# A chunk-wise LRU head with its adaLN sums beside the first blocks, and a Hyena convolution with packed outer stages and rows asked for ahead

## The chip, the cores and the metric

The kernel runs on one core of one Trainium2 chip. The metric is device time in microseconds, the median of three runs. In the rows, PE is TensorE's matrix work, PEld its weight loads, DVE VectorE, ACT ScalarE, POOL GpSimd and SP SyncE; SPq and ACTq are DMA queues by the engine that issues them.

## The reference, cut to what matters

```python
for i in range(DEPTH):                      # DEPTH 2: layer 0 RG-LRU, layer 1 Hyena
    sh1, sc1, g1, sh2, sc2, g2 = split(silu(c) @ ada_w[i] + ada_b[i], 6)   # context: silu(c_ctx)
    u = rms_norm(x, norm_g[i, 0]) * (1 + sc1) + sh1
    ...
    x = x + g1 * y                          # y from the mixer
    x = x + g2 * (relu(modulate(x, ..., sh2, sc2) @ w1) ** 2 @ w2)
# RG-LRU: z = u @ w_in + b_in; gate = gelu(z[:W]); xl = conv4(z[W:]) by rows of 64
# r, i = sigmoid(xl @ w_a), sigmoid(xl @ w_i) by heads, two directions; scans; (hf + hb) * gate @ w_out
# Hyena: z = conv3(u @ w_in + b_in); v, x1, x2 = split(z, 3)
v = x1 * long_conv(v, k_f[:, 0], skip[0])   # long_conv: irfft(rfft(v, 2L) * k_f)[:L] + v * skip
v = x2 * long_conv(v, k_f[:, 1], skip[1])
return v @ w_out + b_out
```

D is 1024, there are 1024 latent tokens (two chunks of 512, c = 0 and 1) and 256 context tokens (chunk c = 2).

## The kernel before, in words

**Products.** A float32 product of the GEMMs is made of three passes on rounded operands: `mm3` (L135 to L137) multiplies whi by uh, whi by ul and wlo by uh. `load` brings a weight block of 512 KB into one of two `raw` buffers (L113), ScalarE rounds it to `whi` (L115), VectorE makes the rest `wlo` (L117). `gemm2` (L154) does two chunks side by side. The Hyena convolution multiplies in full float32: such a matmul of 512 columns is two instructions in the trace.

**Head.** `filter_pos` computes the features of the Hyena filter. `ada_first` (L160 to L185) makes the shift and scale sums of both conditionings (M=2, one PSUM tile for each half, L174) for j = 0 and 1, eight weight tiles each, and transposes the two rows of the result (L181). `norm_apply` modulates the three chunks: a multiply on VectorE (L288), the modulation on ScalarE (L290), the rounding on ScalarE (L291), the rest ul on VectorE or GpSimd (L292). Then the list `TOKENS` (L472) gives the order of the LRU's work: Xhm is an input block (all three chunks with one weight, then a convolution along the tokens on VectorE, L527, and its rounding), Zhm a gate block, Uhm the recurrent gates, Ejx the gate sum j of adaLN: eight 512 KB tiles weighted and added on VectorE (L659, L661), then reduced over partitions by matmuls (L664).

**Hyena long convolution.** Four units u (order o, chunk c) of 16 row blocks. `s1` (L864) turns V into the first transform stage, one 128x128 float32 matmul for each half m of block g; ScalarE copies it to `e` (L866) and a DMA puts it into eight rows of `BIG[u]`, rows `prow(2g+m)` and every fourth behind it. A loop over 64 steps does `fstep` (the filter's spectrum ft by L974, the signal's by L979, four VectorE products L983 to L986, one GpSimd sum L993) and, LAG = 3 steps later, `bstep` (L998, ScalarE copy L999 back to BIG). `s2p` fetches the rows of BIG by DMA (tile e2, L957) and multiplies them by `md` (L958). Inside unit u, the list `side` holds s2p of unit u-1 (8 calls) and s1 of unit u+1 (8 calls), spread over the steps; unit 3 has `back` (transposes L1015 and products L1016) in place of s1. s1 of unit 0 sits in the in-projection before the loop, s2p of unit 3 and half of `back` in the out-projection behind it.

## Time and profile before

| | |
|---|---|
| median of 3 runs | 2819.17 us (2819.03 to 2819.62) |
| profiled execution | 2820.53 us |
| its span | 2818.8 us |
| PE busy | 2664.5 us, 95% |
| DVE / ACT / POOL busy | 1519.5 / 1045.7 / 256.6 us |

The span is the time between the first and the last recorded instruction; 1.73 us of the profiled execution lie around it. Where PE is busy the whole time, only less work on PE can shorten a stretch; where it stands, the row of the next matmul names what it waited for.

### The profile page before, as it was taken

The page shows a single profiled execution, that of the slowest core. Times are in us where ns is not written, and L with a number is a line of the kernel's source. Part 1 is how long each engine was busy: PE and PEld are TensorE (multiplying, and loading weights), DVE is VectorE, ACT ScalarE, POOL GpSimd, SP SyncE. Part 2 cuts the span into 40 slices and gives each one's busy share as a digit, 9 for nine tenths or more (in the row PEclk, how much of TensorE's full clock was granted, in tenths as well). Part 3 has the DMA queues.
Part 4 walks back from the last instruction along what each step waited for, and adds up shares of the span by engine and source line. Part 5 has one row for each costly group of instructions (what it writes and reads, how often), then busy time and mean ns, then how long its engine had stood idle before and what let it go on. Part 6 is the DMA issues. An engine that isn't in the chain of part 4 may idle for free. (4 is left out here: it accounts for less than half of the span.)

```text
span 2818.8 us, 30100 instructions
## 1 busy us (share of the span) xinstructions
PE 2664.5 (95%) x11578; PEld 2027.9 (72%) x11578; DVE 1519.5 (54%) x2077; ACT 1045.7 (37%) x1566; POOL 256.6 (9%) x162
## 2 busy tenths in 40 slices
PE   6689898999999999999999998889799999999998
PEld 1577777878777777778787763333588888888887
DVE  7665665874554554554843447547485333333336
ACT  5557577552333333322622233323353221112213
POOL 0223333010000000000100013212000000000000
PEclk8789999999999999999999999999999999999999
DMA  8331122342443443431313235555421111111112
GB/s 302 124 123 40 50 75 100 117 129 75 135 134 114 142 133 110 135 114 57 120 56 111 83 123 150 139 162 160 134 83 48 51 47 51 45 53 45 53 45 97
DMA packets 120272, 286.28 MB, mean 102 GB/s; under 512 B 11898, under 2 KB 27900, under 8 KB 120002
## 3 DMA queue, kind: packets, MB, share of 16 engines
q1 hardware_dynamic: 109618, 261.30, 29.5%
q10 hardware_dynamic: 8256, 14.68, 1.8%
q0 software_dynamic: 2256, 8.39, 0.9%
q8 instruction: 91, 1.49, 0.2%
q14 instruction: 51, 0.42, 0.0%
HBM read 212.76 MB, written 37.75 MB: 89 GB/s over the span
## 5 line engine op out<-in xcount | busy, mean ns | idle before, releaser
L154 PE MATMUL ps<-u,whi 128*128 128x512 f32 x2696 | 733.5, 392 | 0.0
L115 ACT CAST whi<-raw 128x1024 fp32r<-128x1024 f32 x206 | 216.7, 1052 | 1130.8 <-PE ps L154 1033.5
L154 PEld LDWEIGHTS ps<-u,whi 128*128 128x128 f32 x2696 | 504.1, 188 | 114.6 <-DVE x L789 4.2
L117 DVE TENSOR_TENSOR wlo<-raw,whi 128x1024 fp32r<-128x1024 f32 x206 | 262.1, 1272 | 468.7 <-ACT whi L115 467.9
L154 PE MATMUL ps<-u,wlo 128*128 128x512 f32 x1348 | 421.3, 389 | 0.1
L154 PEld LDWEIGHTS ps<-u,wlo 128*128 128x128 f32 x1348 | 252.9, 188 | 53.7 <-DVE wlo L117 0.8
L154 PE MATMUL ps<-hh,whi 128*128 128x512 f32 x896 | 290.6, 393 | 0.0
L154 PE MATMUL ps<-hh,wlo 128*128 128x512 f32 x896 | 288.4, 389 | 0.0
L154 PE MATMUL ps<-hl,whi 128*128 128x512 f32 x896 | 287.7, 390 | 0.0
L154 PEld LDWEIGHTS ps<-hh,whi 128*128 128x128 f32 x896 | 168.2, 188 | 51.4 <-DVE x L789 11.1
L136 PE MATMUL ps<-u,whi 128*128 128x512 f32 (+1 forms) x508 | 195.4, 386 | 3.7 <-POOL u L292 3.1
L135 PE MATMUL ps<-u,whi 128*128 128x512 f32 (+1 forms) x508 | 187.3, 385 | 11.5 <-ACT u L291 11.5
L137 PE MATMUL ps<-u,wlo 128*128 128x512 f32 (+1 forms) x508 | 193.1, 382 | 1.8 <-DVE wlo L117 1.8
L154 PEld LDWEIGHTS ps<-hh,wlo 128*128 128x128 f32 x896 | 168.1, 188 | 35.2
L154 PEld LDWEIGHTS ps<-hl,whi 128*128 128x128 f32 x896 | 167.9, 188 | 33.8
L789 DVE SCALAR_TENSOR_TENSOR big<-ps,mod,big 128x512 f32<-128x512 f32 (+1 forms) x132 | 91.7, 731 | 185.2 <-PE ps L154 177.7
L789 DVE SCALAR_TENSOR_TENSOR x<-ps,mod,x 128x512 f32<-128x512 f32 x128 | 91.4, 747 | 132.8 <-PE ps L154 124.9
L415 DVE TENSOR_TENSOR ht<-ps,ht 128x512 f32<-128x512 f32 x64 | 44.0, 687 | 162.9 <-PE ps L137 162.9
L292 POOL TENSOR_TENSOR u<-nu,u 128x512 fp32r<-128x512 f32 x24 | 33.9, 1412 | 990.6 <-ACT u L291 981.4
L135 PEld LDWEIGHTS ps<-u,whi 128*128 128x128 f32 x508 | 98.0, 194 | 30.1 <-ACT u L291 12.3
L136 PEld LDWEIGHTS ps<-u,whi 128*128 128x128 f32 x508 | 98.2, 193 | 25.6 <-POOL u L292 6.4
L137 PEld LDWEIGHTS ps<-u,wlo 128*128 128x128 f32 x508 | 97.7, 192 | 20.3 <-DVE wlo L117 3.0
(228 smaller groups left out, 3798.2 us busy)
## 6 DMA issues: line engine op xcount, KB each, us to landing
raw<-in_mlp_w_dram SPq DMA_DIRECT2D x136, 512.0 KB
adaw<-in_ada_w_dram SPq DMA_DIRECT2D x112, 256.0 KB
fd<-fe SPq DMA_DIRECT2D x64, 256.0 KB
ft<-fd SPq DMA_DIRECT2D x64, 256.0 KB
e<-big SPq DMA_DIRECT2D x64, 256.0 KB
eraw<-in_ada_w_dram SPq DMA_DIRECT2D x24, 512.0 KB
raw<-in_hy_w_in_dram SPq DMA_DIRECT2D x24, 512.0 KB
big<-e ACTq DMA_DIRECT2D x48, 256.0 KB
```

What stands on the lines that cost most here:

```text
L115: lsplit[0] = nc.scalar.copy(hi, raw)
L117: lsplit[1] = nc.vector.tensor_tensor(lo, raw, hi.bitcast(F32), op=ALU.subtract)
L135: first = pin(nc.tensor.matmul(ps, wh, rh, start=start, stop=False))
L136: pin(nc.tensor.matmul(ps, wh, rl, start=False, stop=False))
L137: pin(nc.tensor.matmul(ps, wl, rh, start=False, stop=stop))
L154: nc.tensor.matmul(pp[c], x, y[c][k], start=first, stop=last)
L292: applied[k % 2] = (nc.vector if k % 2 else nc.gpsimd).tensor_tensor(ul[k], u, uh[k].bitcast(F32), op=ALU.subtract)
L415: nc.vector.tensor_tensor(ht, ps, ht, op=ALU.mult)
L789: last[0] = nc.vector.scalar_tensor_tensor(xs[m][:, cs], ps[:, :n], g2[:, m:m + 1], xs[m][:, cs], op0=ALU.mult, op1=ALU.add)
```

## The change

It has two halves.

**LRU head.** `ada_first` puts four M=2 matmuls of a pair of weight tiles at four places in one PSUM tile (rows 0, 32, 64, 96), and `finish` adds the halves. Loads come in the order x chunk 0, adaLN tiles and the other chunks; three weight blocks are split at once, and the token B00 takes the place of X00, X01 and Z00: chunk by chunk, for each k three blocks. Half of the tiles of chunk 0 (a quarter of the others) are modulated on VectorE. The filter's matrix `hp` is built later, in `filter_mat`; the fourth filter weight is no longer split ahead and kept in DRAM, but at each use. The sum j = 3 (F, G) lies inside B, j = 4 behind U00, and j = 2 (E00 to E30, in halves of 512) at the end of the LRU.

**Hyena.** `s1` and `s2p` take a pair of blocks gp at a time, as eight matmuls of 32 rows by 64 columns and of 64 rows by 32 columns of the array. The matrix of `back` becomes a permutation (a float32 matmul instead of a transpose), `prow` and the layouts of V and of the convolution change to fit, with more and shorter VectorE and ScalarE operations in `use`. `s2load` asks for the rows of two pairs ahead at step LAG, with 12 buffers (4 in the out-projection, asked for at the use); ft is asked for 3 steps ahead with 4 buffers (8 before); the DMAs into BIG all go to SP's queue (before: ACT's in the loop).

```diff
 def prow(g):
-    return 32 * (g >> 2) + (g & 3)
+    return 64 * (g & 1) + 32 * (g >> 3) + (g >> 1 & 3)
...
+            for i in (0, 1):
+                for h in range(2):
+                    r = 64 * i + 32 * h
+                    nc.tensor.matmul(pp[j][r:r + 2, :], cond[:, :, k - 1 + i], ws[k - 1 + i][:, h * 512:(h + 1) * 512], start=(k == 1), stop=(k == NT - 1))
...
+                if inplace and (k % 2 == 0 if even else k % 4 == 1):
+                    nc.vector.tensor_scalar(u, t, scale[:, k:k + 1], shift[:, k:k + 1], op0=ALU.mult, op1=ALU.add)
+                else:
+                    nc.scalar.activation(u, t, AF.Identity, scale=scale[:, k:k + 1], bias=shift[:, k:k + 1])
...
-    TOKENS = ("X00 X01 E20 Z00 E30 U00 E40 A00 X10 S00 Z01 U01 A01 X11 S01 "
+    TOKENS = ("B00 U00 F40 G40 A00 X10 S00 Z01 U01 A01 X11 S01 "
...
-              "Z30 U30 A30 Z31 U31 " + " ".join(f"Y{k}{c}" for k in range(6) for c in range(2)) + " S30 A31 S31")
+              "E00 Z30 E10 U30 A30 Z31 E20 U31 E30 " + " ".join(f"Y{k}{c}" for k in range(6) for c in range(2)) + " S30 A31 S31")
...
+            def B(h, m):
...
+                for c in range(3):
+                    n = 3 if c < 2 else 2
...
+                    for k in range(NT):
+                        for i in range(n):
+                            mm[0] = gemm(pp[i], w0[i], 0, uh[c], ul[c], [k], NT)
...
+                F(3, 0)
+                for i in range(2):
+                    mix(0, i, zz[i])
+                G(3, 0)
...
-            def s2p(u, g):
+            rows_ = {}
+
+            def s2load(u, gp, pool=cA, bufs=12):
+
+                ee = rows_[u, gp] = []
+                for n in range(2):
+                    for m in range(2):
+                        e = pool.tile([P, 512], F32, tag="e2", name=nm("e2"), bufs=bufs)
+                        b = prow(4 * gp + 2 * n + m)
+                        nc.sync.dma_start(e, BIG[u][b:b + 29:4])
+                        ee.append(e)
+
+            def s2p(u, gp):
...
+                for r in range(2):
+                    rows = slice(64 * r, 64 * r + 64)
+                    for n in range(2):
+                        for m in range(2):
+                            k = 2 * m + r
+                            k = 3 - k if n else k
+                            pin(nc.tensor.matmul(po[n][32 * k:32 * k + 32], md[rows], ee[2 * n + m][rows], start=True, stop=True))
...
-                        pin(nc.tensor.transpose(pt[:, gg * P:(gg + 1) * P], V[c][:, 4 * g4 + gg, j * P:(j + 1) * P], ident))
+                        pin(nc.tensor.matmul(pt[:, gg * P:(gg + 1) * P], V[c][:, 4 * g4 + gg, j * P:(j + 1) * P], pm[:, gg % 2], start=True, stop=True))
...
+                            def both(u, g):
+                                if g == 0:
+                                    s2load(u, 2)
+                                elif g == 1:
+                                    s2load(u, 3)
+                                s2p(u, g)
+                            side += [lambda g=g, u=u: both(u - 1, g) for g in range(4)]
...
+                    if f == LAG and u:
+                        s2load(u - 1, 0)
+                        s2load(u - 1, 1)
...
+                    s2load(3, m, cp[0], 4)
+                    s2p(3, m)
```

The next two pieces are TensorE's order in the head. In the kernel before, each row is an instruction (with the tile that it writes, the tile that it streams or holds, and the output's size): the end of X01, the j = 2 sum's matmuls into pst, the start and end of Z00, the j = 3 sum, the start and end of U00, and the j = 4 sum ahead of X10's context chunk.

```order
L137 MATMUL ps_177_843<-u_143_504,wlo_173_788 128x256
L664 MATMUL pst_190_907<-ones_77,eacc_181_882 128x1 x8
L135 MATMUL ps_195_924<-u_104_465,whi_192_919 128x512
L136 MATMUL ps_195_924<-u_112_473,whi_192_919 128x512
...
L137 MATMUL ps_196_950<-u_127_488,wlo_193_921 128x512
L664 MATMUL pst_206_1001<-ones_77,eacc_197_976 128x1 x8
L135 MATMUL ps_211_1018<-xh_169_780,whi_208_1013 128x512
L136 MATMUL ps_211_1018<-xl_170_782,whi_208_1013 128x512
...
L137 MATMUL ps_220_1083<-xh_179_878,wlo_209_1015 128x256
L664 MATMUL pst_233_1140<-ones_77,eacc_224_1115 128x1 x8
L135 MATMUL ps_240_1172<-u_136_497,whi_237_1167 128x256
```

In the changed kernel, B's first rows, its last, the j = 3 sum ahead of U00 and the j = 4 sum ahead of X10:

```order
L135 MATMUL ps_165_699<-u_2_116,whi_101_338 128x512
L135 MATMUL ps_166_700<-u_2_116,whi_104_344 128x512
L135 MATMUL ps_167_701<-u_2_116,whi_107_350 128x512
L136 MATMUL ps_165_699<-u_10_124,whi_101_338 128x512
L137 MATMUL ps_165_699<-u_2_116,wlo_102_340 128x512
L136 MATMUL ps_166_700<-u_10_124,whi_104_344 128x512
...
L137 MATMUL ps_172_856<-u_41_155,wlo_105_346 128x256
L762 MATMUL pst_188_958<-ones_77,eacc_173_907 128x1 x8
L135 MATMUL ps_193_975<-xh_183_941,whi_190_970 128x512
...
L137 MATMUL ps_202_1040<-xh_186_954,wlo_191_972 128x256
L762 MATMUL pst_215_1097<-ones_77,eacc_206_1072 128x1 x8
L135 MATMUL ps_222_1129<-u_34_148,whi_219_1124 128x256
```

Three weight blocks (whi_101, whi_104, whi_107) now share each u, and two sums instead of three stand between the first GEMM and X10.

In the loop, the rows of TensorE around the first s2p of a middle unit stand in this order before (y is a step's product, mi its inverse matrix, m21 a forward one):

```order
L974 MATMUL ps_2383_12660<-ft_2382_12658,m21_12183 128x512
L979 MATMUL ps_2385_12664<-big_2188_12181,m21_12183 128x512
L958 MATMUL ps_2389_12674<-e2_2390_12675,md_12194 128x512
L958 MATMUL ps_2389_12674<-e2_2391_12678,md_12194 128x512
L958 MATMUL ps_2393_12683<-e2_2394_12684,md_12194 128x512
L958 MATMUL ps_2393_12683<-e2_2395_12687,md_12194 128x512
L998 MATMUL ps_2396_12691<-y_2364_12615,mi0_12186 128x512
L974 MATMUL ps_2398_12696<-ft_2397_12694,m21_12183 128x512
```

And in the changed kernel, with L1122 for the filter's spectrum, L1133 for the signal's, L1152 for the inverse and L1101 for s2p (the four rows shown are the first of eight):

```order
L1122 MATMUL ps_2396_12931<-ft_2371_12875,m21_12421 128x512
L1152 MATMUL ps_2398_12935<-y_2362_12854,mi0_12424 128x512
L1133 MATMUL ps_2399_12938<-big_2192_12419,m21_12421 128x512
L1122 MATMUL ps_2404_12950<-ft_2379_12894,m21_12421 128x512
L1101 MATMUL pst_2410_12962<-e2_2383_12903,md_12432 32x512
L1101 MATMUL pst_2410_12962<-e2_2384_12905,md_12432 32x512
L1101 MATMUL prb_2411_12963<-e2_2385_12907,md_12432 32x512
L1101 MATMUL prb_2411_12963<-e2_2386_12909,md_12432 32x512
L1152 MATMUL ps_2413_12975<-y_2370_12873,mi0_12424 128x512
L1133 MATMUL ps_2414_12978<-big_2192_12419,m21_12421 128x512
L1122 MATMUL ps_2419_12990<-ft_2395_12929,m21_12421 128x512
```

Four full matmuls for two blocks have become eight small ones, in the two PSUM tiles that pst and prb use; the filter's spectrum stands one step ahead of the signal's.

SP's queue at the same place, before, with L970 for the filter's rows and L957 for those of BIG:

```order
L970 DMA ft_2452_12832<-fd_81 128x512
L970 DMA ft_2468_12871<-fd_81 128x512
L957 DMA e2_2390_12675<-big_2041_11178 128x1x512
L957 DMA e2_2391_12678<-big_2041_11178 128x1x512
L957 DMA e2_2394_12684<-big_2041_11178 128x1x512
L957 DMA e2_2395_12687<-big_2041_11178 128x1x512
L957 DMA e2_2405_12711<-big_2041_11178 128x1x512
L957 DMA e2_2406_12714<-big_2041_11178 128x1x512
L970 DMA ft_2484_12910<-fd_81 128x512
L970 DMA ft_2500_12949<-fd_81 128x512
L957 DMA e2_2408_12719<-big_2041_11178 128x1x512
L957 DMA e2_2409_12722<-big_2041_11178 128x1x512
```

And in the changed kernel (L1116 and L1087):

```order
L1116 DMA ft_2395_12929<-fd_80 128x512
L1116 DMA ft_2403_12948<-fd_80 128x512
L1087 DMA e2_2383_12903<-big_2053_11372 128x1x512
L1087 DMA e2_2384_12905<-big_2053_11372 128x1x512
L1087 DMA e2_2385_12907<-big_2053_11372 128x1x512
...
L1087 DMA e2_2409_12960<-big_2053_11372 128x1x512
L1116 DMA ft_2418_12988<-fd_80 128x512
L1087 DMA e2_2421_12994<-big_2053_11372 128x1x512
```

The rows of BIG came in sixes and fours between filter rows; now twelve stand in one piece, and the next filter row waits behind them.

## Rows read from the trace of the kernel before

**Rows 1.** The page, part 1: busy time, share of the span, instructions.

```profile
PE 2664.5 (95%) x11578; PEld 2027.9 (72%) x11578; DVE 1519.5 (54%) x2077; ACT 1045.7 (37%) x1566; POOL 256.6 (9%) x162
```

**Rows 2.** Windows: PE, PEld, DVE, ACT, POOL busy; granted clock, DMA share, GB/s.

```profile
0.00:80.00 80.00, 45.56 (x113) 13.26 (x114) 53.36 (x140) 50.80 (x88) 3.34 (x8) 0.80 0.78 272
80.00:171.00 91.00, 72.00 (x313) 60.08 (x312) 61.19 (x56) 37.64 (x62) 19.96 (x14) 0.78 0.48 150
171.00:480.00 309.00, 279.10 (x1302) 232.81 (x1303) 195.12 (x130) 210.74 (x249) 105.12 (x35) 0.94 0.19 60
...
1664.00:1983.40 319.40, 275.53 (x608) 113.02 (x606) 202.28 (x295) 106.99 (x187) 82.82 (x67) 0.95 0.55 159
```

**Rows 3.** The same view, two short windows.

```profile
6.50:42.00 35.50, 25.15 (x63) 7.63 (x64) 24.75 (x71) 19.43 (x35) 0.00 (x0) 0.84 1.03 383
2012.00:2016.00 4.00, 4.00 (x19) 3.12 (x18) 1.23 (x1) 1.40 (x3) 0.00 (x0) 1.00 0.70 225
```

**Rows 4.** Timeline of PE in the head: start, duration, group [idle before <- releaser].

```profile
79.60 1.22 PE L135 MATMUL ps<-u,whi 128*128 128x512 f32 x2 [11.54 <-ACT u L291]
...
144.90 0.77 PE L135 MATMUL ps<-xh,whi 128*128 128x512 f32 x1
...
159.93 0.39 PE L136 MATMUL ps<-xl,whi 128*128 128x512 f32 x1
160.15 0.39 PE L137 MATMUL ps<-xh,wlo 128*128 128x512 f32 x1
...
167.56 3.54 PE L664 MATMUL pst<-ones,eacc 128*128 128x1 f32 x16 [6.31 <-DVE eacc L661]
170.97 0.56 PE L135 MATMUL ps<-u,whi 128*128 128x256 f32 x1
```

**Rows 5.** Timeline of ACT before the first GEMM.

```profile
66.86 10.68 ACT L290 ACTIVATE xl<-xl,mod,scl 128x512 f32<-128x512 f32 x15 [0.67 <-DVE scl L303]
```

**Rows 6.** Lines of DVE, 0 to 300 us: count | busy, mean ns | idle <- releasers.

```profile
L527 DVE SCALAR_TENSOR_TENSOR xc<-z,vec,xc 128x1008 f32<-128x1008 f32 (+3 forms) x30 | 34.3, 1154 | 0.2
L661 DVE SCALAR_TENSOR_TENSOR eacc<-eraw,cond,eacc 128x1024 f32<-128x1024 f32 x21 | 28.9, 1376 | 21.8 <-DMA eraw<-in_ada_w_dram 21.5 <-DVE xc L527 0.2
```

**Rows 7.** Timeline of PE at the filter's packed stage.

```profile
702.83 1.09 PE L432 MATMUL ps<-ht,mf 32*32 32x512 f32 x16
703.85 0.50 PE L154 MATMUL ps<-hh,whi 128*128 128x512 f32 x1
```

**Rows 8.** Timeline of PE in the convolution loop.

```profile
1664.49 1.02 PE L979 MATMUL ps<-big,m 128*128 128x512 f32 x2
1665.35 1.88 PE L864 MATMUL ps<-v,m 128*128 128x512 f32 x4
...
1722.72 1.02 PE L979 MATMUL ps<-big,m 128*128 128x512 f32 x2
...
1725.29 1.02 PE L979 MATMUL ps<-big,m 128*128 128x512 f32 x2
...
1733.02 1.02 PE L979 MATMUL ps<-big,m 128*128 128x512 f32 x2
...
1771.56 1.02 PE L979 MATMUL ps<-big,m 128*128 128x512 f32 x2
...
1812.65 1.02 PE L979 MATMUL ps<-big,m 128*128 128x512 f32 x2
...
1906.07 1.02 PE L979 MATMUL ps<-big,m 128*128 128x512 f32 x2
```

**Rows 9.** Waits of PE, 0 to 300 and 1664 to 1983: total, times, longest.

```profile
PE pst L664 <- DVE eacc L661: 17.1, 3, 6.3
...
PE ps L958 <- DMA e<-big: 24.9, 23, 5.0
```

**Rows 10.** Timeline of PE in the out-projection.

```profile
2035.54 1.03 PE L1015 MATMUL ps<-ident,v 128*128 128x128 f32 x8
2036.33 0.71 PE L154 MATMUL ps<-yh,whi 128*128 128x512 f32 x2
```

More of the change, by code (lines that the diff above doesn't have):

```diff
@@ L96, in tile_block @@
     hpd = dram.tile([16, P, 2, P], F32, name="hpd")
-    w4d = dram.tile([4, P, 2, 512], F32, name="w4d")
     fd = dram.tile([4, 16, P, 512], F32, name="fd")
@@ L187, in ada_half @@
+        return [lambda j=j, k=k: step(j, k) for j in range(2) for k in range(NT)], finish
     def ada_half(pool, l, j, h):
@@ L387, in fetch @@
             w = fp.tile([P, 2, 512], F32R, tag="w4", name=nm("w4"), bufs=2)
-            nc.sync.dma_start(w.bitcast(F32), w4d[u])
+            raw = fp.tile([P, 512], F32, tag="fe", name=nm("w4r"), bufs=2)
+            nc.sync.dma_start(raw, a["fw4"][:, u * 512:(u + 1) * 512])
+            nc.scalar.copy(w[:, 0], raw)
+            nc.vector.tensor_tensor(w[:, 1], raw, w[:, 0].bitcast(F32), op=ALU.subtract)
             st["w4", u] = w
@@ L530, in lru, with F, G @@
             XC, GT = {}, {}
+            mm, mixed, sums = [None], [copied], {}
+            def F(j, _):
+                acc = sums[j] = lt.tile([P, T], F32, tag="hf" if j == 3 else "g", name=nm("eacc"), bufs=1 if j == 3 else 2)
+                with tc.issue_after(mixed[0].ins):
+                    for k in range(NT):
+                        w = wp_[0].tile([P, 1024], F32, tag="raw", name=nm("eraw"), bufs=2)
+                        nc.sync.dma_start(w, a["ada_w"][0, k * P:(k + 1) * P, j * D:(j + 1) * D])
+                        if k == 0:
+                            nc.vector.tensor_scalar(acc, w, cond[:, 0, k:k + 1], None, op0=ALU.mult)
+                        else:
+                            nc.vector.scalar_tensor_tensor(acc, w, cond[:, 0, k:k + 1], acc, op0=ALU.mult, op1=ALU.add)
+            def G(j, _):
+                with tc.issue_after(mm[0].ins):
+                    ada_sum(j, sums.pop(j))
             cols = (slice(0, 512), slice(512, T), slice(T, T + TC))
@@ L949, in load_mi @@
                 nc.gpsimd.dma_start(mi[q], a["mi"][:, 4 * q:4 * q + 4])
-            def s2p(u, g):
-                o, c = units[u]
-                po = psum()
-                for m in range(2):
-                    e = cp[0].tile([P, 512], F32, tag="e2", name=nm("e2"), bufs=6)
-                    b = prow(2 * g + m)
-                    nc.sync.dma_start(e, BIG[u][b:b + 29:4])
-                    pin(nc.tensor.matmul(po, md[:, m], e, start=(m == 0), stop=(m == 1)))
-                if o == 0:
-                    if g == 0:
-                        V[c] = vtile()
-                    nc.vector.tensor_tensor(V[c][:, g], po, X1[c][:, g], op=ALU.mult)
-                else:
-                    nc.scalar.copy(V[c][:, g], po)
+            rows_ = {}
@@ new lines, in hyena, with fload, kstep @@
+            kks, fts = {}, {}
+            def fload(i):
+                if i < 64:
+                    fts[i] = cA.tile([P, 512], F32, tag="ft", name=nm("ft"), bufs=4)
+                    nc.sync.dma_start(fts[i], fd[i // 16, FORD[i % 16]])
+            def kstep(i):
+                j, ft = i % 16, fts.pop(i)
+                pk = psum()
+                pin(nc.tensor.matmul(pk, m2[j // 4][:, j % 4, 64:192], ft, start=True, stop=True))
+                kk = cpool.tile([P, 512], F32, tag="kk", name=nm("kk"), bufs=3)
+                nc.scalar.copy(kk, pk)
+                kks[i] = kk
@@ L1026, in hyena @@
             pinned[0] = True
+            for i in range(3):
+                fload(i)
+            kstep(0)
             for i in range(64 + LAG):
@@ L1037, in hyena @@
                         if u > 0:
[L1038 removed]
+                            def both(u, g):
[5 more added lines that the diff above has]
+                            side += [lambda g=g, u=u: both(u - 1, g) for g in range(4)]
                         if u < 3:
[L1040 removed]
+                            side += [lambda g=g, u=u: s1(u + 1, g) for g in range(4)]
                         else:
```

295 lines of the change are left out of this document (178 added, 117 removed).

## The prediction

> **What bounds the kernel now.** I read the page first: TensorE is busy 95% of the span [rows 1]. So time can only come from two places: stretches where TensorE stands, and work on TensorE that goes away. The second view, busy time by stretch, says where it stands [rows 2]: 34 us of the first 80, 19 us of the next 91, 30 us from 171 to 480, and 44 us of the 319 of the long-convolution loop (1664 to 1983). The rest is the MLPs and projections, which the change leaves as they are but for the pieces below.
>
> In the head the timeline shows why it stands [rows 4]. The first token matmul starts at 79.60, after 11.54 us of waiting for ScalarE's rounded u. Later TensorE stops three times for a gate sum on VectorE, 17.1 us together [rows 9]; the last, of 6.31, stands ahead of X10. The first X10 matmul starts at 170.97; I measure the head to there. ScalarE is the late engine before the first GEMM: it modulates the chunks one behind the other from 66.86 [rows 5]. Early on the loads are the limit: 383 GB/s from 6.5 to 42 [rows 3].
>
> In the loop, each of the 64 frequency steps issues three fp32 pairs (L974, L979, L998), 2.57 us together (1722.72 to 1725.29) [rows 8]. On top come the outer stages: s2p (L958) and s1 (L864), each matmul two instructions and 0.86 us (1664.49 to 1665.35). The first L979 of each unit stands at 1664.49, 1722.72, 1812.65 and 1906.07, and the loop ends at 1983.4: 58.2, 89.9, 93.4 and 77.3 us. Unit 1 spends 10.3 us before its first s2p, 38.5 us in the s2p part (1733.02 to 1771.56) and 41.1 us in the s1 part. The waits name its s2p: 23 waits on the DMA e<-big, 24.9 us [rows 9].
>
> **Part 1, the head: -38 us.** Loads up to the last adaLN tile and the first weights are about 13 MB; by [rows 3] that is 34 us after 6.5, so the last tile lands at about 40. Then come the sum of the strips, the transposes, the first modulated tile and three weight splits, of which the third has to wait for a raw buffer: first GEMM at 53 (48 if nothing queues, 58 if the splits do), against 79.6. Two things make this possible: chunk 0 alone is now in front of it, and half its modulation goes to VectorE. B then does the work of X00, X01 and Z00, k by k. Two full chunks are 72 matmuls each at 0.23 us, or 16.4; the context is 48 at 0.12, or 5.6. (The start of one such row to the next is 0.22 in U00, 159.93 to 160.15, which runs from 144.90 to 161.2.) That gives 38.5 us: B ends at 91 if the tiles keep up, and a TensorE at the low clock, as the 0.80 and 0.78 of [rows 2] say it partly is here, adds some us. Before, the same work lay before U00's start at 144.90, with two stops in it. Now the mix of two blocks falls in one piece between B and U00: 6 latent convolution operations of 1.15, the context's, two roundings and what is left of the j=3 sum (8 x 1.38), some 16 to 20 us on VectorE with nothing for TensorE to do [rows 6]. U00 starts at about 107 (before: 144.9), runs 16 us, and waits for the j=4 sum: eight loads at 2.6 us (28.9 us of work and 21.8 of waits over 21 in [rows 6]), to about 133. X10 at 133 instead of 171: **-38**, bounds -52 (48, and the j=4 loads come early) and -25 (58, and mix in full behind B).
>
> **Part 2, the j=2 sum at the end of the LRU: +3 us** (0 to +6). It is 11 us of VectorE (16 halves of 0.69) put where VectorE feeds TensorE. VectorE is busy 195 of 309 us between 171 and 480 [rows 2], so most of it is covered; without that cover it costs 11.
>
> **Part 3, s1 of the first unit, inside the in-projection: -9.3 us.** There TensorE has no idle to hide in. 16 matmuls of 0.86 are 13.7 us; 4 packed groups take their place. The nearest row to such a group is the filter's L432: 8 fp32 matmuls of 32x32 on the array in 16 instructions, 702.83 to 703.85 until the next GEMM, 1.02 us [rows 7], where 16 full instructions at 0.43 would be 6.9. So 4 x 1.09 = 4.4. [...]
>
> **Part 4, the loop: -66 us.** Per unit 16 steps remain (41.2 us), and the four s1 or s2p matmuls of a pair (3.43) become one group of 1.05. Unit 0: its 16 s1 (13.7 us) become 4.2: **-9.5**. Units 1 and 2: the first 10.3 us stay. The s2p part is now paced by loads alone: eight rows are asked for at step 3 and the rest behind them into 12 buffers, all 16 at 256 KB. The loop as it is moves 159 GB/s with 0.55 of the engines [rows 2], and the out-projection's loads and weights together 225 [rows 3]; between them, at 195, a load takes 1.34 us, 16 take 21.5, and with the first one's flight 23.4. The s1 part needs 8 steps and 4 groups (24.8 us), and 16 writes of 1.34 from its second step on (28 in all with copy and flight): I take 32, as writes and loads now share SP's queue, and 41.1 was the price before. That is 66: **-24** and **-27**. Unit 3 has s2p only, and `back` with its transposes, now matmuls: 71 for 77.3, **-6**. Two bounds. VectorE's 202 us in the loop [rows 2] does not change, so nothing beyond -115 can come. If SP's queue, in which a load that waits for a buffer now holds ft and the writes behind it, gives half back, -30.
>
> **Part 5, the out-projection: +3 us.** Its 4 packed s2p groups give 9.6 back (16 x 0.86 to 4 x 1.05), but e2 has only 4 buffers there, all asked for at the group itself: about 2 us of load latency each, +7.5. `back`'s 32 transposes there become fp32 matmuls: 8 transposes take 0.8 us [rows 10], 8 such matmuls at a quarter of a 512-column pair (0.21) take 1.7: +4, and perhaps double with their new weights. Sum about +3.
>
> **Sum.** -38 + 3 - 9.3 - 66 + 3 = -107. The profiled execution took 2820.53 us, 1.73 more than its span and 1.4 more than the median of 2819.17; a difference carries over unchanged: 2819.17 - 107 = **2712 us**.
>
> **Rivals.**
> *Rows at both halves' rate.* `prow` now alternates neighbouring row groups between partitions below and above 64; before, eight in a row lay in one half. The DMA share in the loop stands near a half, 0.55 [rows 2]. If consecutive rows went to different engines, both the s2p and the s1 parts would fall towards their matmuls: about -8 in three s2p parts and -4 in two s1 parts, -33: 2679. Against it: 0.70 of the engines at 225 GB/s is the best such stretch [rows 3], with other traffic in it. Chance 0.18. [...]
>
> *SP's one queue.* It now carries loads, ft and writes in program order. A write waits for ScalarE's copy; the ft three steps on waits behind it. If each of the 20 side groups of units 1 to 3 loses 1.5 us so, +30, and the head may give up six more with its weights behind x: about 2748. For it: L970 and L957 stand in SP's queue already. Against: ft now has three steps, 7.7 us, of lead. Chance 0.24.
>
> *Packed groups that don't run side by side (slower).* If the 32x64 and 64x32 tiles go one behind the other, a group costs 8 x 0.86 = 6.9 us, twice what its four matmuls cost before. Outside the loop that is 8 x 5.8 = +46 against the forecast; in the loop units 1 and 2 become 96 us of matmuls instead of 66, unit 0 69 for 48.7, unit 3 74 for 71: +83. In all 2841, slower. It decides from about 6 us a group. L432's row speaks against it. Chance 0.04.
>
> *Nothing gained.* Head and loop both give back what they win, in the mix gap and the queue: 0.02.
>
> **How the numbers follow.** Forecast 0.52, own range 2692 to 2732; both halves 0.18 (2665 to 2692); SP's queue 0.24 (2732 to 2775); slower 0.04; nothing 0.02. The likeliest gives 2712. From 2662 to 2762 about 0.12 is left out above (the slower one, nothing, and the tail of the queue) and 0.05 below. A measurement of this kernel can tell about 0.2%, 5.6 us, from no change; faster 0.94, same 0.02, slower 0.04.
>
> **What would show it.** First token matmul near 53 and first X10 matmul near 133; a gap of 10 to 20 us before U00; s1 and s2p groups of 16 instructions in about 1.05 us; units of about 49, 66, 66 and 71 us; the waits on e<-big in the loop down to a few us. The forecast is wrong if the groups are longer than 2 us, if the s2p part stays above 30 us, if L979 or L974 begin to wait for DMAs, if the mix holds U00 beyond 120, or if the units fall below 58.

## The result and the profile after

The changed kernel takes 2777.3 us (median of 4 runs, 2775.28 to 2787.04), the kernel before, on the same chip, 2819.1: 0.986 of it, 95% interval 0.9836 to 0.9884. That is faster by 1.4%, clear of the noise: 42 us where 107 were forecast, and outside the range of 2662 to 2762. The profiled execution's span is 2775.7 us, 43.1 less than before.

The page's first part, as in [rows 1]:

```profile
PE 2620.3 (94%) x11898; PEld 1994.5 (72%) x11898; DVE 1564.4 (56%) x2226; ACT 1054.9 (38%) x1627; POOL 262.8 (9%) x166
```

The span fell by 43.1 us and TensorE's work by 44.2; its idle time, some 155 us, which the forecast wanted to shorten as well, is as long as it was. The same windows as in [rows 2], the last one now the loop's new place:

```profile
0.00:80.00 80.00, 40.53 (x162) 20.82 (x163) 64.58 (x147) 49.29 (x87) 12.72 (x14) 0.87 0.61 213
80.00:171.00 91.00, 71.21 (x337) 61.48 (x336) 65.31 (x65) 50.33 (x72) 21.56 (x14) 0.83 0.44 139
171.00:480.00 309.00, 278.28 (x1302) 233.24 (x1301) 203.13 (x145) 204.72 (x244) 104.41 (x35) 0.93 0.24 80
1644.60:1938.60 294.00, 257.52 (x831) 90.98 (x829) 200.27 (x293) 103.60 (x186) 81.07 (x64) 0.92 0.55 165
```

The loop's traffic per second hardly rose (165 GB/s, 159 before), at the same DMA share of 0.55. TensorE's timeline in the head: the first token matmul, the j = 3 sum with its wait, U00, the j = 4 sum and X10:

```profile
65.90 1.65 PE L135 MATMUL ps<-u,whi 128*128 128x512 f32 x3 [3.73 <-ACT u L306]
...
119.40 3.57 PE L762 MATMUL pst<-ones,eacc 128*128 128x1 f32 x16 [12.00 <-DVE eacc L587]
122.83 2.69 PE L135 MATMUL ps<-xh,whi 128*128 128x512 f32 x6
...
145.72 3.54 PE L762 MATMUL pst<-ones,eacc 128*128 128x1 f32 x16 [7.13 <-DVE eacc L587]
149.12 0.56 PE L135 MATMUL ps<-u,whi 128*128 128x256 f32 x1
```

X10 starts at 149.12, 21.9 us earlier than in [rows 4] and 16 later than forecast. TensorE's timeline around the loop: the filter's spectrum (L1122) and a stall ahead of the loop's first step, a packed s1 group of 16 instructions (first and last shown) up to the next matmul, and the first L1133 of units 0 to 3 and the loop's last row:

```profile
1642.81 2.07 PE L1122 MATMUL ps<-ft,m 128*128 128x512 f32 x2 [4.54 <-ACT v L1051]
1644.68 1.91 PE L1133 MATMUL ps<-big,m 128*128 128x512 f32 x2
...
1654.86 0.64 PE L968 MATMUL pst<-v,m 32*64 32x512 f32 x1
...
1655.39 0.59 PE L968 MATMUL ps<-v,m 32*64 32x512 f32 x1
1655.91 1.12 PE L1152 MATMUL ps<-y,mi 128*128 128x512 f32 x2
...
1693.74 1.02 PE L1133 MATMUL ps<-big,m 128*128 128x512 f32 x2
...
1772.73 1.10 PE L1133 MATMUL ps<-big,m 128*128 128x512 f32 x2 [1.68 <-issue]
...
1857.51 1.10 PE L1133 MATMUL ps<-big,m 128*128 128x512 f32 x2 [1.77 <-DMA ft<-fd]
...
1937.51 1.12 PE L1152 MATMUL ps<-y,mi 128*128 128x512 f32 x2 [1.70 <-POOL y L1147]
```

The units take 49.1, 79.0, 84.8 and 81.1 us (58.2, 89.9, 93.4 and 76.5 before): unit 0 gained as forecast, units 1 and 2 less than half as much as forecast, and unit 3 lost 4.6 us. Both loops are taken to the end of their last matmul here. For the kernel before that is 1982.6, by this row of TensorE, and not the 1983.4 of the prediction:

```profile
1981.48 1.13 PE L998 MATMUL ps<-y,mi 128*128 128x512 f32 x2 [1.70 <-POOL y L993]
```

Stretch by stretch, from the places in the two timelines (us):

| stretch | forecast | measured |
|---|---|---|
| head, to X10 | -38 | -21.9 |
| j = 2 sum at the LRU's end | +3 | +5.4 |
| in-projection, to the loop's start | -9.3 | -3.2 |
| loop | -66 | -24.2 |
| out-projection | +3 | +0.8 |
| span | -107 | -43.1 |

### The profile page after: what moved, and what is told of

It is laid out like the page before. It is cut to its first block, busy times and chain, and to the rows that moved or that the text cites. A ratio compares the mean times of both kernels' runs of the same rounds, so it can differ in the third digit from the quotient of the medians.

```text
span 2775.7 us, 30992 instructions
## 1 busy us (share of the span) xinstructions
PE 2620.3 (94%) x11898; PEld 1994.5 (72%) x11898; DVE 1564.4 (56%) x2226; ACT 1054.9 (38%) x1627; POOL 262.8 (9%) x166
## 4 chain that ended last, share of the span: by engine, by line
PE 76%; DVE 9%; DMA 6%; ACT 5%; issue 2%; SPq 1%; POOL 1%; DVEq 0%; ACTq 0%; POOLq 0%
PE ps L154 57%; PE ps L135 4%; PE ps L136 4%; PE ps L137 4%; DMA e<-big 3%; DMA big<-e 1%; PE ps L455 1%; DVE xc L571 1%; PE ps L1152 1%; PE ps L1122 1%; PE ps L1133 1%; DVE hf L716 1%; DMA eraw<-in_ada_w_dram 1%; ACT T L653 1%; ACT r L653 1%
## 5 line engine op out<-in xcount | busy, mean ns | idle before, releaser
L154 PEld LDWEIGHTS ps<-hl,whi 128*128 128x128 f32 x896 | 167.9, 188 | 33.8
```

The lines of the kernel that those rows point to most:

```text
L154: nc.tensor.matmul(pp[c], x, y[c][k], start=first, stop=last)
```

## The experiments

All are edits of the changed kernel. Times are medians; the ratio is to runs of the kernel before on the same chip, so kernels of different chips are compared by it. "s2p part" is the second quarter of a unit's steps, where rows of BIG come in, "s1 part" its second half. Places in single profiles scatter: in the eight profiles that do the same work up to the loop (the changed kernel and the seven that edit only the loop) it starts between 1642.8 and 1647.3, and in the seven with an unchanged loop the loop takes 290.6 to 297.2 us. Smaller differences show nothing.

### The loop: is it the transfer of rows?

**l_rows_dram** fetches each row block from a contiguous place in DRAM; the dependence of s2p on BIG is left out, and with it the wait for the last row written.

```diff
-                        nc.sync.dma_start(e, BIG[u][b:b + 29:4])
+                        nc.sync.dma_start(e, fd[u, 4 * gp + 2 * n + m])
```

> Edit of the changed kernel: the rows for s2p are fetched from a contiguous block in DRAM instead of from eight partitions of BIG; same number of transfers, bytes, buffers and queue. It leaves out the data flow from BIG to s2p (and with it the wait for the last row written). Theory (the s2p parts are paced by 256 KB transfers that keep half of the DMA engines busy, about 2 us each): a load spread over all engines takes about 1 us or less, each s2p part (33 to 38 us now) falls to about 18 to 22, the loop from 294 to about 245, total -45 us (-30 to -55). Rival (SP's one queue in program order sets the pace): the queue is the same, s2p parts stay above 28 us, total at most -12.

Measured: 2727.64 us, 0.969 [0.967, 0.9709]; the loop falls from 293.9 to 250.2 us, the s2p parts from 33.3, 37.6 and 34.6 to 19.7, 16.6 and 20.9. The DMA view of the s2p part of unit 1, 40 slices (busy share in tenths of 16 engines, and GB/s), first of the changed kernel, then of this one:

```profile
DMA  5555545555555555965555555579678855588541
GB/s 156 142 149 142 144 124 141 146 142 132 142 141 142 137 137 149 226 134 132 141 149 141 144 154 154 151 174 308 139 276 199 251 142 196 199 246 276 196 164 37
```

```profile
DMA  7650019597978799720000016999988879899999
GB/s 79 245 208 0 0 33 337 175 133 308 374 258 241 254 354 329 300 92 8 0 0 0 0 50 141 374 383 270 237 308 266 275 229 225 295 378 349 345 349 366
```

With rows from BIG most slices show 130 to 150 GB/s at 5 tenths, with the same bytes from DRAM up to 380 at 9 tenths; over the windows that is 165 GB/s at a share of 0.59, and 214 at 0.67. The theory holds: the middle units are paced by the rows' transfer.

**l_old_prow** and **l_pool_rows** ask whether a half of SBUF or the number of engines sets that rate: the first keeps `prow` (and its inverse) as it was before, the second sends every second row block by GpSimd's queue.

```diff
-    return 64 * (g & 1) + 32 * (g >> 3) + (g >> 1 & 3)
+    return 32 * (g >> 2) + (g & 3)
```

```diff
-                        nc.sync.dma_start(e, BIG[u][b:b + 29:4])
+                        (nc.gpsimd if m else nc.sync).dma_start(e, BIG[u][b:b + 29:4])
```

> Edit of the changed kernel, undoing one part: the row map prow of the kernel before (eight neighbouring blocks in one half of the partitions), with the constants that fit it. Theory (neither half nor alternation decides, the number of engines of one transfer does): total 0 (-5 to +5). Rival of the prediction (alternating halves is what makes loads faster): s2p parts longer by 5 us each or more, total +15 or more.

> Edit of the changed kernel: of the rows for s2p, every second is asked for by GpSimd's queue, the others by SP's. Theory (the row loads on SP's queue all use the same half of the engines): if GpSimd's loads use other engines, the s2p parts fall from 33-38 us to about 22, the DMA share in them rises well over 0.6, total -30 us (-15 to -40). If they use the same half: s2p parts as now, total 0 to +10 (GpSimd's sums wait behind its issues).

Measured: 2780.13 us, 0.9865 [0.9845, 0.9885], s2p parts 32.3, 37.0 and 33.8; and 2785.83 us, 0.9884 [0.9869, 0.9898], s2p parts 33.1, 37.0 and 33.3. The row map makes no difference, so the rival of both halves falls. The same DMA view of l_pool_rows:

```profile
DMA  5555579999999999999994559995965588555840
GB/s 139 127 134 139 127 214 199 149 134 137 127 127 122 161 196 214 179 201 129 161 169 117 162 140 258 184 171 72 204 202 129 137 196 254 117 191 194 283 176 0
```

In stretches the busy share is nearly twice as high (9 tenths) and mostly the same bytes arrive; over the window 162 GB/s at a share of 0.81, against 165 at 0.59 in the changed kernel. So the number of engines falls too. What sets the rate, no run isolates.

**l_rows_pieces** brings each row block in four pieces of 64 KB, so that at one time other target partitions are written (the rows come out in another order).

```diff
-                        nc.sync.dma_start(e, BIG[u][b:b + 29:4])
+                        for j in range(4):
+                            (nc.scalar if j % 2 else nc.sync).dma_start(e[32 * j:32 * j + 32], BIG[u][b:b + 29:4, 4 * j:4 * j + 4])
```

> Edit of the changed kernel: each 256 KB row load for s2p is cut into four transfers of 64 KB, one for each 32 partitions of its target, alternately from SP's and ScalarE's queue; the order inside the tile changes with it (the rows arrive permuted, so s2p multiplies other rows; bytes and matmuls stay). [...] Rival (the rate is that of the source's eight partitions, or the issue of four times as many transfers): s2p parts at 33 us or more, total 0 to +20.

Measured: 2776.02 us, 0.9861 [0.9842, 0.9881]. The s2p parts fall to 27.2, 27.7 and 24.3 us, below the rival's 33, with the same eight source partitions; the s1 parts of units 1 and 2 grow to 42, and what the loop gains (it takes 286.3 us) is lost in the out-projection, so the total stays. The pieces differ in three things at once: the target partitions in flight, their size, and the second queue. A second queue alone (GpSimd's) did nothing in l_pool_rows; whether the target or the size makes the rate is not shown.

**l_act_writes** gives the writes to BIG back to ScalarE's queue, as they were: the rival of SP's one queue.

```diff
-                        nc.sync.dma_start(BIG[u][b:b + 29:4], e)
+                        (nc.scalar if cp[0] else nc.sync).dma_start(BIG[u][b:b + 29:4], e)
```

> Edit of the changed kernel, undoing one part: the writes into BIG inside the loop go to ScalarE's queue again. Theory (half of the DMA engines set the pace): who asks doesn't matter, total 0 (-5 to +5), the s1 parts stay at 35 to 37 us. Rival (SP's one queue, in which a write that waits for its copy holds the filter rows and loads behind it): total -10 to -25 us, the s1 parts at 28 us or less.

Measured: 2789.01 us, 0.9908 [0.9891, 0.9924]; the loop takes 305.7 us, 11.8 more, with s1 parts of 38.3 and 39.0. For the writes the rival is refuted: SP's queue is the better place, and the loop lies clear of the scatter.

### Unit 3: the loads in one piece

In unit 3 all four s2p groups stand at steps 4 to 7. **u3_spread** sets them at steps 6, 8, 10 and 12 and `back` behind them; **u3_spread_ft_act** moves ft to ScalarE's queue as well.

```diff
-                    while len(side) > ns - min(ns, -(-ns * (f - f0 + 1) // (14 - f0))):
+                    due = sum(f >= t for t in (6, 8, 10, 12, 13, 14, 14, 15)) if u == 3 else min(ns, -(-ns * (f - f0 + 1) // (14 - f0)))
+                    while len(side) > ns - due:
```

```diff
-                    nc.sync.dma_start(fts[i], fd[i // 16, FORD[i % 16]])
+                    nc.scalar.dma_start(fts[i], fd[i // 16, FORD[i % 16]])
```

> Edit of the changed kernel: in unit 3 the four s2p calls stand at steps 6, 8, 10 and 12 and the four calls of back behind them, instead of one at each of steps 4 to 11; the row loads are asked for with their calls as before. Theory (TensorE, which works in order, stands in front of each s2p while the rows come in at about 2 us each, and later has steps without any transfer): unit 3 from 81 us to about 66, total -13 us (-6 to -18). Rival (steps late in the unit have no slack; VectorE is the limit there): 0 to -4.

> The spread s2p of unit 3 as before, and the filter rows asked for through ScalarE's queue instead of SP's. Theory (with s2p spread, TensorE waited for the filter rows, 5.9, 2.7 and 5.5 us, which stand behind row loads of 2 us each in the same queue): unit 3 from 79 to about 66, units 1 and 2 a few us shorter too, total -13 us against the changed kernel (-6 to -22). Rival (the bytes through half of the DMA engines set the pace whoever asks, as with the writes on ScalarE's queue): 0 to +10.

u3_spread: 2775.93 us, 0.9859 [0.984, 0.9879], no gain. The s2p waits are gone, but TensorE now waits for the filter's rows, which stand behind the row loads in SP's queue:

```profile
1883.75 2.04 PE L1122 MATMUL ps<-ft,m 128*128 128x512 f32 x2 [5.88 <-DMA ft<-fd]
1902.54 1.40 PE L1122 MATMUL ps<-ft,m 128*128 128x512 f32 x2 [2.71 <-DMA ft<-fd]
1916.33 2.04 PE L1122 MATMUL ps<-ft,m 128*128 128x512 f32 x2 [5.49 <-DMA ft<-fd]
```

With ft in another queue: 2769.63 us, 0.9826 [0.9812, 0.9841]; unit 3 takes 69.1 us and the loop 279.4. The interval of the ratio still touches that of the changed kernel, but in all five kernels with both edits (this one and the four combos below) unit 3 takes 69.1 to 72.0 us and the loop 277.4 to 285.1. So the rival of SP's one queue is right for this place. It has a part in unit 2 too: its s2p part takes 32.7 to 34.6 us in these five, and 35.0 to 39.3 in the eleven kernels that fetch the same whole rows from BIG with ft in SP's queue.

### The head: what holds U00 and X10?

**h_mult_after** lets VectorE's multiplies of the later chunks wait behind the first chunk's modulation. **h_hpd_pool** stores the filter's matrix by GpSimd's queue, **h_filter_early_pool** builds that matrix early besides, as before.

```diff
-            nc.vector.tensor_tensor(t, x, rb, op=ALU.mult)
             u = x if inplace else pool.tile([P, 512], F32, tag="nu", name=nm("nu"), bufs=2)
             with ExitStack() as order:
                 for ins in after:
                     order.enter_context(tc.issue_after(ins.ins))
+                nc.vector.tensor_tensor(t, x, rb, op=ALU.mult)
```

```diff
-            nc.sync.dma_start(hpd[:, :, n].rearrange(
+            nc.gpsimd.dma_start(hpd[:, :, n].rearrange(
```

```diff
-                with tc.issue_after(rounded[0].ins), tc.issue_after(applied[0].ins), tc.issue_after(applied[1].ins):
-                    copied = filter_mat(fs, h)
...
                 for step in first:
                     step()
+                copied = filter_mat(fs, h)
```

> Edit of the changed kernel: the multiplications that normalise chunk 1 and the context on VectorE are ordered behind chunk 0's rounding, as their modulation already is. Theory (in the head the additions that finish the shift and scale sums stand in VectorE's queue behind 16 of those multiplications, 7.6 us, and behind the weight splits): first token matmul at about 57 instead of 65.9, the rest of the head moves with it, total -9 us (-5 to -13). Rival (the first GEMM waits for weights and loads): first token matmul stays above 62, total 0 to -4.

> Edit of the changed kernel: the two stores of the filter matrix (hpd) go to GpSimd's queue instead of SP's. New theory of the head (SP's queue stands from 59 to 96 us behind these stores, which wait for ScalarE's and GpSimd's splits; the j=3 sum's loads 3 to 8 and the recurrent gates' weight are queued behind them, so VectorE waits 12 us with the convolution of B behind it): U00 from 122.8 to about 115, first X10 matmul from 149 to about 141, total -8 us (-4 to -12). Old theory (what counts is when the first token matmul starts): it stays at 66, so total 0 (-3 to +3).

> Edit of the changed kernel: the filter matrix (filter_mat) is built right behind the filter's features, as in the kernel before, instead of behind the last chunk's rounding, and its two stores go to GpSimd's queue. Theory (two things hang on these stores: the buffer z of B, which takes their source's memory, and, in SP's queue, the loads of the j=3 sum): the stores are over before B's first result, ScalarE no longer waits for them, the j=3 sum is done earlier; U00 from 122.8 to about 115, X10 from 149 to about 141, total -8 us (-3 to -12). Rival (the head's length is VectorE's own work, and filter_mat now takes VectorE and ScalarE ahead of the shift and scale sums): first token matmul later by 3 to 6 us, total 0 to +5.

Measured: 2780.88 us, 0.9879 [0.9865, 0.9894]; 2784.69 us, 0.9873 [0.9857, 0.989]; 2774.71 us, 0.9855 [0.9839, 0.9872]. None gains what was expected. In the first, the first token matmul moves from 65.90 to 61.57 and U00 all the same to 124.34. B loses the 4.3 us again, in one stop for ScalarE's z and in the matmuls behind it, which run at a granted clock of 0.69 (to 108.70; 1.00 in the changed kernel from 73.60 on):

```profile
100.46 0.58 PE L135 MATMUL ps<-u,whi 128*128 128x256 f32 x1 [4.26 <-ACT z L631]
```

This z takes the memory from which the filter's matrix is stored, and ScalarE waits 5.2 us for that store, as in the changed kernel, where B was later and did not notice. In the second, the wait grows to 12.0 us: a later store holds z longer. In the third, the first token matmul falls back to 72.59, and U00 still comes at 120.70. The chain of waits of the changed kernel shows why one edit does so little (start, duration, what; pieces left out at the dots):

```profile
90.86 5.35 POOL hp L391 x4
...
96.70 6.84 DMA eraw<-in_ada_w_dram
103.64 1.30 DVE eacc L587
...
111.75 1.28 DVE eacc L587
113.03 1.23 DVE xc L571 x2
...
114.98 1.20 DVE eacc L587
116.18 0.75 DVE xc L571
...
120.92 1.40 DVE xl L614
...
124.86 0.66 DVE eacc L585
125.55 4.59 DMA eraw<-in_ada_w_dram
130.23 1.29 DVE eacc L587
```

Six of the eight j = 3 tiles are asked for only at 96.70, behind the stores of the filter's matrix, and each of their products stands in VectorE's queue between two convolutions (L571) of the mix; then the j = 4 tiles start the same again. VectorE stands 12.34 us for the first of the six, but beside B's last matmuls. Two chains of nearly one length, that of the blocks and that of the filter's matrix and the tiles, meet in VectorE.

**h_short_sums** adds only two of the eight tiles in each of the two sums (the other six are left out).

```diff
-                    for k in range(NT):
+                    for k in range(2):
                         w = wp_[0].tile([P, 1024], F32, tag="raw", name=nm("eraw"), bufs=2)
```

> Edit of the changed kernel: the j=3 and j=4 sums take two of their eight tiles; it leaves out twelve loads of 512 KB and twelve VectorE operations of 1.28 us. Theory (the two sums, one behind the other through two buffers, set U00 by 6 and X10 by 7 us of waiting): U00 from 122.8 to about 113, X10 from 149 to about 133, total -10 to -16 us. Rival (VectorE's convolution and the LRU's own chain behind it set the end; the sums fill gaps): X10 earlier by less than 5, total 0 to -4.

Measured: 2762.27 us, 0.9804 [0.9772, 0.9836]. U00 starts at 112.92, and neither sum's matmuls wait any more:

```profile
108.80 1.84 PE L762 MATMUL pst<-ones,eacc 128*128 128x1 f32 x16
...
112.92 1.77 PE L135 MATMUL ps<-xh,whi 128*128 128x512 f32 x6 [2.28 <-ACT xh L612]
...
130.07 0.28 PE L135 MATMUL ps<-u,whi 128*128 128x256 f32 x1
```

X10 begins at 130.07, right behind U00 and ahead of the j = 4 sum's matmuls, and that with the first token matmul at 67.68; the loop starts 16.6 us earlier. So the two sums hold some 19 us of the path. The forecast had priced 21 for them (8 x 1.38 ahead of U00, 10 behind it), so this is what could still be saved in the head and not what the forecast missed.

**combo_3** and **combo_4** (with the edits of u3_spread_ft_act) set one or both sums behind later blocks, each sum's loads and matmuls together:

```diff
-    TOKENS = ("B00 U00 F40 G40 A00 X10 S00 Z01 U01 A01 X11 S01 "
+    TOKENS = ("B00 U00 A00 X10 F40 G40 S00 Z01 U01 A01 X11 S01 "
```

```diff
-    TOKENS = ("B00 U00 F40 G40 A00 X10 S00 Z01 U01 A01 X11 S01 "
+    TOKENS = ("B00 U00 A00 X10 F30 G30 S00 Z01 U01 A01 X11 F40 G40 S01 "
...
-                F(3, 0)
...
-                G(3, 0)
```

> Edit of the changed kernel: spread s2p in unit 3 and filter rows on ScalarE's queue (2769.6 us alone), and the j=4 sum moved from between U00 and A00 to behind X10. Theory (the place of the sum costs, not its work): X10 from 149 to about 140, total 2762 us (2757 to 2766). Rival (VectorE's 10 us and the loads cost the same there): 2768 to 2773.

> As combo_3, but both sums are moved: j=3 from inside B to behind X10, j=4 to behind X11. Theory (the place costs): U00 at about 113, X10 at about 131 to 135, total 2756 us (2750 to 2762). Rival (VectorE is busy enough in the LRU that the work costs what it did): 2768 to 2775.

Measured: 2793.89 us, 0.9925 [0.9903, 0.9947], and 2819.13 us, 1.0012 [1.0002, 1.0021]. X10 comes as forecast, at 139.66 and 130.56. Yet both lose, 24 us and 50 in the medians against u3_spread_ft_act, by one long stop for each sum that was moved, here that of combo_3:

```profile
193.74 3.55 PE L762 MATMUL pst<-ones,eacc 128*128 128x1 f32 x16 [39.42 <-DVE eacc L587]
```

In combo_4 there are two, of 34.89 and 38.79. Most of the loads start only behind the new block's mix, and the sum's matmuls stand next in TensorE's order: moving both together carries the stop along.

**combo_7** sets them apart: the matmuls of j = 3 behind U00, the loads of j = 4 behind X10's place in the list but free to start at B's mix, and its matmuls behind Z01.

```diff
-    TOKENS = ("B00 U00 F40 G40 A00 X10 S00 Z01 U01 A01 X11 S01 "
+    TOKENS = ("B00 U00 G30 A00 X10 F40 S00 Z01 G40 U01 A01 X11 S01 "
...
-                with tc.issue_after(mixed[0].ins):
+                with tc.issue_after((mixed[0] if j == 3 else sums[0]).ins):
...
-                G(3, 0)
+                sums[0] = mixed[0]
```

> u3_spread_ft_act (2769.6 us) plus another place in the head: the loads of the second sum's tiles (j=4) are issued before the second chunk's mix, but its matmuls stand several steps later in TensorE's order, and no other step waits for them; nothing of the computation is left out. Theory (a sum whose loads and matmuls stand far apart is hidden): X10 starts near 140 us instead of 149, the in-projection loop starts some 7 us earlier, total near 2762 us (2756 to 2768). Rival (VectorE's products of the sum wait in its in-order queue for the 512 KB loads, and the LRU's own chain stands behind them): X10 may come early but the blocks behind it wait, total 2772 to 2795 us.

Measured: 2763.49 us (2762.11 to 2763.85), 0.9812 [0.9796, 0.9828]: the lowest median of the whole computation. TensorE's timeline: U00's start, X10's first row, and the two sums without a wait:

```profile
120.72 2.72 PE L135 MATMUL ps<-xh,whi 128*128 128x512 f32 x6 [14.43 <-ACT whi L115]
...
135.38 0.28 PE L135 MATMUL ps<-u,whi 128*128 128x256 f32 x1
...
138.13 1.84 PE L762 MATMUL pst<-ones,eacc 128*128 128x1 f32 x16
...
163.25 1.84 PE L762 MATMUL pst<-ones,eacc 128*128 128x1 f32 x16
```

X10 at 135.38 instead of 152.37 in u3_spread_ft_act; the loop starts 7.3 us earlier (1640.0 and 1647.3), and takes 284.5 us, within what it takes in the five kernels with this loop. By ratio the step is 4 us, and the two intervals overlap, so its size is not settled; against the changed kernel the intervals are apart.

**combo_1** joins h_mult_after, h_filter_early_pool and u3_spread_ft_act.

> All that helped or should help, together: filter matrix early with its stores on GpSimd's queue, chunk 1's and the context's normalisation behind chunk 0, spread s2p in unit 3 and filter rows on ScalarE's queue. Theory (the parts add up): head -10, loop -13 against the changed kernel, about 2754 us (2745 to 2764). Rival (only the loop part counts, the head ends where it did): 2762 to 2772.

Measured: 2767.31 us, 0.9833 [0.9819, 0.9848], which can't be told from u3_spread_ft_act alone. The first token matmul is back at 66.46 with the early filter matrix, and U00 is at 120.07: the gains of the head's edits do not add.

### The small terms

**c_plain_copy** copies the blocks of V and X1 in one ScalarE instruction instead of five, and so leaves out the exchange of partitions. **e_short_sum** takes one tile of eight in the j = 2 sum.

```diff
-                    nc.scalar.copy(dv[:, 0], pv[:, 0])
-                    for r in range(4):
-                        (nc.scalar.copy if r % 2 else nc.vector.tensor_copy)(dv[96 - 32 * r:128 - 32 * r, 1], pv[32 * r:32 * r + 32, 1])
+                    nc.scalar.copy(dst[c][:, 4 * g4:4 * g4 + 4, o:o + P], pt.rearrange("p (g d) -> p g d", g=4))
```

```diff
-for k in range(NT) if 0 < step < 3 else ():
+for k in range(1) if 0 < step < 3 else ():
...
-for k in range(NT) if step < 2 else ():
+for k in range(1) if step < 2 else ():
```

> Edit of the changed kernel: the transposed blocks of V and X1 are copied by one ScalarE copy each, as before, instead of one and four quarters on ScalarE and VectorE; it leaves out the exchange of partitions, so V's blocks stand in the old order. Theory (the in-projection kept 6 of the 9.3 us that packed s1 takes off it, because the last blocks' copies stand between VectorE's convolution pieces and hold PSUM, 4.5 us of waiting ahead of the loop): the loop starts 4 to 6 us earlier, total -5 us (-3 to -8). Rival (the stall is the last block's convolution, not the copies): 0 to -2.

> Edit of the changed kernel: the j=2 sum at the end of the LRU takes one of its eight tiles for each half; it leaves out 14 loads of 256 KB and 14 VectorE operations of about 0.7 us. Theory (the sum, put where VectorE feeds TensorE, costs about 5 us, the difference from X10 to the end of the LRU): total -3 to -7 us. Rival (it lies beside TensorE's work and the 5.4 us come from elsewhere): 0 to -2.

c_plain_copy: 2776.84 us, 0.9864 [0.9845, 0.9884]; the loop starts at 1639.0, 5.7 us earlier, and the 4.54 us stall ahead of it is gone, which stands with that same length in seven of the other profiles; the loop takes 296.7, within its scatter, and the total shows nothing. e_short_sum: 2780.04 us, 0.9867 [0.9834, 0.9901]; in its profile the loop starts at 1640.9, 3.8 us earlier. Neither can be told from the changed kernel by its time. That the stall is gone is shown; the 3.8 us are within the scatter's width (1.9 under the lowest other start), so the size of the j = 2 term is not settled.

## Why the prediction was right in direction and wrong in size

**Head, -38 forecast, -21.9 measured: the term that failed is "first GEMM at 53".** The first token matmul came at 65.90, outside the term's own bounds of 48 and 58, and these 12.9 us are most of the 16 by which X10 came late. The other terms came out nearly as forecast. B took 41.5 us, to 107.40 (38.5 forecast, and some more allowed for the low clock): TensorE did not wait in it, but for its first 7.7 us the granted clock was 0.61, 1.00 from then on. The gap before U00 was 15.4 us (16 forecast) and of the kind that was forecast: VectorE has j = 3 products and two blocks' convolutions to do. From U00 to X10 it was 26.3 (26 forecast); the eight j = 4 products start 2.6 us apart (124.86 to 145.58), as forecast, but by luck: the row that the forecast names gives (28.9 + 21.8) / 21 = 2.4.

Why the first matmul is late is shown in part. The rows of adaLN (L188) stand in VectorE's queue behind the multiplies of a chunk (L297), here the first of four in VectorE's timeline:

```profile
46.08 4.87 DVE L297 TENSOR_TENSOR xl<-xl,prb 128x512 f32<-128x512 f32 x8
...
52.64 0.69 DVE L188 TENSOR_TENSOR arow<-ps,arow 2x512 f32<-2x512 f32 x1
```

h_mult_after takes the multiplies out of the way and wins 4.3 of the 12.9 us; where the rest goes, no run isolates. It also shows a second limit that the forecast did not name: the filter's matrix, which the change itself moved later, whose stores hold ScalarE's z and, in SP's queue, the j = 3 tiles. An earlier first matmul ran into it and X10 gained nothing. So whether a start at 53 would have brought X10 to 133 is not shown.

**j = 2 sum, +3 forecast, +5.4 measured.** In its bounds of 0 to +6; e_short_sum, with 3.8, agrees in sign.

**Packed groups, right.** 1654.86 to 1655.91 is 1.05 us for 16 instructions of 32x64, and an s2p group whose rows are there runs from 1961.75 to 1962.74:

```profile
1961.75 1.06 PE L1101 MATMUL pst<-e,md 64*32 64x512 f32 x8
1962.74 0.72 PE L154 MATMUL ps<-yh,whi 128*128 128x512 f32 x2
```

So [rows 7], with 1.02 us, was the right neighbour, and the rival that would have been slower, with 6.9 us a group, falls. Unit 0, which of the outer stages has only s1, gained 9.1 us (9.5 forecast).

**In-projection, -9.3 forecast, -3.2 measured.** The matmuls fell as forecast; the new, shorter copies of V and X1 came to the path instead: 4.54 us of stall ahead of the loop, which is gone without them. The section on the change names these operations; the forecast put them at nothing.

**Loop, -66 forecast, -24.2 measured: the term that failed is 1.34 us for a load.** It came from an interpolation, 195 GB/s between two windows whose traffic is of other kinds. The s2p part of unit 1 takes 33.3 us for 16 loads, 2.08 us each. In it a group of s2p, 1.05 us where its rows are there, waits for one row after the other; the first runs from its first matmul to the L1152 behind it, 9.1 us, the other three 3.5 to 4.4:

```profile
1706.41 1.04 PE L1101 MATMUL pst<-e,md 64*32 64x512 f32 x2 [0.38 <-DMA e<-big]
...
1715.51 1.88 PE L1152 MATMUL ps<-y,mi 128*128 128x512 f32 x2
```

TensorE's waits for rows in the whole loop, as in [rows 9], for the two PSUM tiles of s2p:

```profile
PE prb L1101 <- DMA e<-big: 13.0, 17, 1.5
PE pst L1101 <- DMA e<-big: 5.8, 7, 2.4
```

That is 18.8 us, where [rows 9] has 24.9 and the forecast a few: much of what the faster groups save goes into waiting. For units 1 to 3 the s2p parts account for 9.9, 14.2 and some 11 us of the miss, the s1 parts of units 1 and 2 (35.3 and 36.8 for 32) for 8. The old row, 38.5 us for 16 loads in the s2p part of the kernel before, was in the prediction, at 2.4 us a load; it was read as TensorE's time plus waits. The rate in that window of the kernel before could have been read as well, 138 GB/s, far from 195 (the view of [rows 2]):

```profile
1733.00:1771.50 38.50, 29.66 (x57) 11.02 (x56) 19.64 (x29) 4.69 (x8) 7.61 (x6) 0.91 0.55 138
```

In unit 3 the forecast of 71 met a cost that it did not name: the four groups come early in one piece and `back` behind them, so that nothing covers the rows; spread out, and with ft in another queue, the unit took 69.1.

**Out-projection, +3 forecast, +0.8 measured**, with the wait for rows all in one place, 5.54 us ahead of the first group:

```profile
1944.18 3.65 PE L1101 MATMUL pst<-e,md 64*32 64x512 f32 x8 [5.54 <-DMA e<-big]
```

The 2 us of load latency that the forecast put on each group are shown by no run; this one wait stands in their place.

**Rivals.** Both halves: refuted by l_old_prow. SP's one queue: its time of 2748 was the nearest of all, yet its mechanism held only for ft, in unit 3 and in part in unit 2, and for the tiles behind the filter's stores in the head; for the writes it was the other way round. (Both halves by its own terms is -32 and not -33.) What sets the rows' rate stays open: the same rows in smaller pieces to other target partitions came quicker (27.2 us for 33.3 in unit 1), but source, target and size were never changed one at a time.

## What to carry to other kernels

Where a stage waits for a transfer on both sides of a change, take the transfer's price from that very stage, its part's length over its loads, and not from the average of windows with other traffic (here 2.08 us, and not 1.34). The faster s2p groups beside such a transfer mostly waited, 18.8 us where it was 24.9. The sum j = 3 over tiles that must be fetched stopped two engines, VectorE for 12.34 us where a product waited for its tile and TensorE for 12.00 where the reduction stands: put distance between the request and the use, and look at every order edge on the request when something else in the program is moved. An earlier start of a stage is worth only what the next chain that ends in the stage lets through: in h_mult_after the first token matmul came 4.3 us earlier, and U00 not at all.

## What the runs showed of the hardware

While rows were copied from eight SBUF partitions to 128, most slices of unit 1's s2p part show 130 to 150 GB/s, where with the same bytes from DRAM they reach 380 (l_rows_dram), and a higher busy share of the engines (0.81 against 0.59 over that part, l_pool_rows) brought no more (162 GB/s, 165 without it). A packed group of 16 small matmul instructions took 1.05 us up to the next full matmul (1654.86 to 1655.91). The same loop code takes 290.6 to 297.2 us in seven kernels that differ elsewhere, so a few us in one profile's stretch are no effect.
